# A two-layer decoder trunk on one core: x and the first weights in one array at the opening, the first norm from token rows, and the last product in two column halves

## The chip, the core and the metric

The kernel runs on one core of a Trainium2 chip. It is written in Bass with a tile framework that puts the instructions of each engine in an order at build time; on the chip each engine then runs its own list in that order. The engines are TensorE (PE, with weight loads listed as PEld), VectorE (DVE), ScalarE (ACT), GpSimd (POOL) and SyncE (SP, which here only issues DMAs). The metric is the device time of one execution in microseconds (us), lower is better.

## What is computed

The reference is a decoder trunk of two layers over 256 tokens of width 2048, float32:

```python
h = x
for layer in range(2):
    hn = rms_norm(h, norm_mix[layer])
    mix = recurrent_mixers(hn, ...) if layer % 2 == 0 else dilated_attention(hn, positions, ...)
    h = h + mix
    h = h + squared_relu_mlp(rms_norm(h, norm_mlp[layer]), mlp_w1[layer], mlp_w2[layer])
return rms_norm(h, final_norm)

def rms_norm(x, gain):
    return x * lax.rsqrt(jnp.mean(x * x, axis=-1, keepdims=True) + 1e-6) * gain

def squared_relu_mlp(h, w1, w2):
    return jnp.square(jax.nn.relu(h @ w1)) @ w2
```

Layer 0 mixes with an RG-LRU group and an HGRN2 group behind one input projection, layer 1 with dilated window attention. The width of the MLPs is 8192. Nearly all the arithmetic is matrix products with 256 rows.

## The kernel before

**Numbers and tiles.** A float32 product is made of three matmuls of a faster type: each operand is split into a rounded part and a remainder ("hi" and "lo" for weights, the two halves of bufa or bufb for activations), and hi x hi, hi x lo and lo x hi are summed in PSUM. Weights come as units of 128 x 2048 (1 MB); `fetch` loads one into `raw` (three buffers), ACT casts hi (L104), VectorE subtracts for lo (L105). hi and lo have three buffers each, so a unit's cast waits until TensorE has finished the unit three before. x is split in the same way by `split_to` with the norm's gain (ACT L252, VectorE L253); the norm's factor itself is applied to the products afterwards.

**The opening.** 12 warm-up matmuls on ones (L263) come first on TensorE. `fetch_first` then loads x by features (`xin`, 16 blocks k of 128 features by 256 tokens) and the first four weight units in alternating transfers on SP's queue: pieces of one k for the first unit, of two k's for the second, whole units after that. The first product, `v0` (L191, `tokens` with `by_k`), is 2 token halves x 512 columns over 16 k's: 24 matmuls per weight unit in the order of k, 96 in all. `FirstNorm` squares each block of xin (ACT L284), adds the squares on VectorE (L287, L289) and sums over features with matmuls against ones (L297); VectorE makes rt = 1/sqrt by Newton steps (L334 to L339), ACT scales v0 with it, and two transposes with the identity out of `tab_` (L321) turn it into the row vector `rs` that scales the products of the projections. x by tokens (`xtok`, 2 MB), the residual, is loaded over xin afterwards. All large matmuls are chained in program order (`mm`); small ones, such as those of the recurrence, are placed between them when the program is built. Projections of the recurrence stage take 48 matmuls of 256 columns and one of three PSUM banks.

**The MLP's end.** `blocks` computes two column groups of 512 (n0, n0 + 1) for two token halves j = 0, 1 with seven block products where eight would be plain: units "a", "t1", "t2", "c", "t3", "d", "t4" of 12 matmuls each, and four plain units "n" of 24 (12 for each j). The order is that of `ORDERS`; for w2 it ends t3, d, n 2, t4, n 3. `beta` and `gamma` are the PSUM banks of the first group's j = 1 and j = 0. In the last call (layer 1, q = 3, n0 = 2) column group 2 (`LAST`) is finished last. `to_x` (L769) adds a bank times the norm factor to the residual `xres`, and `Norm.add` (L308) squares 512 columns with a running sum for the final norm.

**The end.** For each j, VectorE and ACT make the final factor (L974 to L983), and four groups of 512 columns are scaled, by ACT (L992) or VectorE (L990, L996). With j = 0 ACT scales groups 0 and 3, with j = 1 groups 0 and 1. The output leaves in four pieces of 512 KB: three on SP's queue, the first half of j = 1 on ACT's.

Of the kernel before, what the change touches and what calls it, by code (L numbers as in the profile page):

```python
# [41 lines left out]
def trunk_kernel(ctx, tc, x, xtok, cols, tab, masks, pos, fin, w_in, w_gate, w_out, w_qkv, w_o, w1, w2, out):  # L42
# [17 lines left out]
    xin = xall.rearrange("p (k s) -> p k s", s=S)  # L60
# [14 lines left out]
    where = {"x": (w_in, lambda i: i, 1), "y": (w_in, lambda i: 8 + i, 1), "g": (w_gate, lambda i: i, 1),  # L75
             "v": (w_in, lambda i: 16 + 16 * i, 4), "h": (w_in, lambda i: 20 + i // 4 * 16 + i % 4 * 3, 3)}
# [16 lines left out]
    class Weights:  # L93
# [7 lines left out]
        def split(self, at, n):  # L101
            h, l = self.part(at, n)
            w = self.raw[:, at:at + n]
            A.copy(h, w)  # L104
            i = V.tensor_tensor(l, w, h.bitcast(F32), OP.subtract)  # L105
            self.ins = getattr(i, "ins", i)
# [4 lines left out]
    def fetch():  # L111
# [5 lines left out]
        with stream():  # L117
# [4 lines left out]
            nc.sync.dma_start(r, src[i])  # L122
# [154 lines left out]
    class FirstNorm:  # L277
        def __init__(self):
            self.ss, self.n = [], 0

        def add(self, blk):
            self.n += 1
            q = wk.tile([P, S], F32, name="t1", bufs=2)
            A.activation(q, blk, AF.Square)  # L284
            if self.n == 1:
                self.ss.append(wk.tile([P, S], F32, name="q", bufs=1))
                V.tensor_copy(self.ss[0], q)  # L287
            elif self.n < KB:
                V.tensor_tensor(self.ss[0], self.ss[0], q, OP.add)  # L289
            else:  # L290
                self.ss.append(q)

        def mean(self):
            p = psc.tile([P, 512], F32, name="pt", bufs=1)
            for j in range(2):
                for i, q in enumerate(self.ss):
                    T.matmul(p[:, 2 * j:2 * j + 1], q[:, j * P:j * P + P], one, start=i == 0, stop=i == 1)  # L297
            m = tmp.tile([P, 2], F32, name="nm2", bufs=2)
            V.tensor_scalar(m, p[:, 0:4:2], 1.0 / D, EPS, op0=OP.mult, op1=OP.add)
            return m  # L300

    class Norm:
        def __init__(self):
            self.ss = tmp.tile([P, 2, 4], F32, name="ss", bufs=2)

        def add(self, j, n):
            q = tmp.tile([P, S], F32, name="z").bitcast(BF16)
            A.activation(q, xres[:, j, n * 512:n * 512 + 512], AF.Square, accum_out=self.ss[:, j, n:n + 1])  # L308
# [51 lines left out]
    def tokens_group(src, i0, rt=None, by_k=False, kgs=(0, 1, 2, 3)):  # L360
        ps = tokens(src, i0, bufa, kgs, by_k)
        v = vgs.tile([P, 2, 512], F32, name="vg")
        with urgent():
            for j in range(2):
                A.activation(v[:, j], ps[j], AF.Copy, scale=1.0 if rt is None else rt[:, j:j + 1])
# [80 lines left out]
    def hgrn_v(i):  # L446
        v = tokens_group(w_in, 16 + i * 16, rt if i else None, by_k=not i)
        if not i:
            for j in range(2):
                A.activation(v[:, j], v[:, j], AF.Copy, scale=rt[:, j:j + 1])  # L450
        return v

    def hgrn(hd, vg):
        u0 = 16 + (hd // 4) * 16 + 4 + (hd % 4) * 3
# [130 lines left out]
    for step in ORDER.split():  # L585
        i = int(step[1])
        if step[0] == "v":
            vgroups[i] = hgrn_v(i)
# [68 lines left out]
    def blocks(src, i0, n0, mov, forms, events, final):  # L657
# [11 lines left out]
        def times(bank, w, get):  # L669
            for i in range(4):  # L670
                h, l = w.part(i * 512, 512)
                xh, xl = get(i)
                mm(bank, xh, h, start=not any(b is bank for b in opened), stop=False, skip_group_check=True)
                opened.append(bank)
                mm(bank, xh, l, start=False, stop=False, skip_group_check=True)
                mm(bank, xl, h, start=False, stop=i == 3, skip_group_check=True)

        plains = [0, 0]
        for what, u in ORDERS[src is not w1]:
            w = unit(src, None if u is None else i0 + 4 * n0 + u)  # L680
            due = len(later)
            if what != "n":
# [433 lines left out]
```

## Time and profile before

| | us |
|---|---|
| median of 3 runs | 2155.81 |
| lowest and highest | 2155.46, 2155.9 |
| the profiled execution | 2155.38 |
| its span, first to last instruction | 2153.4 |

The profile is of one execution. Its span is cut into windows and groups; busy time is what an engine's instructions took, "idle before" what an engine waited ahead of them and for whom. PEclk is the clock that TensorE was granted, as a share of full speed. A DMA is shown where it is issued (SPq, ACTq), and its landing is counted from there. In the timeline a row begins with its start and its duration in us; the starts of two rows of one engine give the pace, since instructions overlap at their ends.

### The profile page before, as it was taken

Reading aid. Unit: us, or ns where it says so; the run is one execution under the profiler, and the core shown is the slowest. Engines: PE = TensorE matmul, PEld = TensorE weight load, DVE = VectorE, ACT = ScalarE, POOL = GpSimd, SP = SyncE. Lnnn points to the kernel's source line nnn. Section 1 sums busy time; section 2 is a strip of 40 time slices with the busy share of each in tenths; the row PEclk is TensorE's granted clock in tenths of the full one; section 3 lists DMA queues with packets and bytes.
Section 4 is the critical chain, followed back from the end, with each engine's and each line's share of the span. In section 5 each row is a group of like instructions: output and inputs, shape, how many; then the busy total and the mean of one; then the engine's idle time right before and its main releaser. Section 6 shows DMA issues by size and latency. Waiting matters only on the chain.

```text
span 2153.4 us, 27729 instructions
## 1 busy us (share of the span) xinstructions
PE 2139.0 (99%) x11020; PEld 1831.6 (85%) x11020; DVE 1787.4 (83%) x2098; ACT 1269.8 (59%) x1415; POOL 61.9 (3%) x77
## 2 busy tenths in 40 slices
PE   9999999999999999999999999999999999999998
PEld 8999998888888888888888888888888888888886
DVE  7776787788888888889998897867988988888887
ACT  7444485566566566557665545456655755755764
POOL 0000000000000000000000000000000000000000
PEclk9999999999999999999999999999999999999999
DMA  8444446578878788887785556457878778788884
GB/s 321 157 157 158 156 157 214 177 233 272 247 243 257 256 248 238 277 247 237 236 271 197 175 159 232 157 185 224 238 239 284 238 241 262 257 246 241 274 257 154
DMA packets 68736, 485.64 MB, mean 226 GB/s; under 512 B 7664, under 2 KB 8432, under 8 KB 10624
## 3 DMA queue, kind: packets, MB, share of 16 engines
q1 hardware_dynamic: 58176, 410.89, 52.0%
q0 software_dynamic: 10144, 72.39, 18.2%
q8 instruction: 86, 1.41, 0.3%
q10 hardware_dynamic: 288, 0.61, 0.1%
q14 instruction: 42, 0.34, 0.0%
HBM read 481.76 MB, written 2.10 MB: 225 GB/s over the span
## 4 chain that ended last, share of the span: by engine, by line
PE 97%; DVE 1%; ACT 1%; DMA 0%; issue 0%; SPq 0%
PE p L191 67%; PE pd L191 13%; PE po L191 12%; PE pl L194 2%; PE pl L487 1%; PE pt L191 1%; DVE lo L105 0%; DMA xall<-in_x 0%; PE pl L883 0%; ACT hi L104 0%; PE po L904 0%; PE pd L896 0%; PE pd L471 0%; PE pl L882 0%; PE po L905 0%
## 5 line engine op out<-in xcount | busy, mean ns | idle before, releaser
L104 ACT CAST hi<-raw 128x2048 fp32r<-128x2048 f32 (+2 forms) x468 | 683.7, 1484 | 546.9 <-PE p L191 343.0
L105 DVE TENSOR_TENSOR lo<-raw,hi 128x2048 fp32r<-128x2048 f32 (+2 forms) x468 | 816.3, 1759 | 218.5 <-ACT hi L104 203.6
L191 PE MATMUL p<-hi,bufb 128*128 128x512 f32 x1408 | 448.8, 391 | 0.5 <-ACT bufb L249 0.5
L191 PE MATMUL p<-hi,bufa 128*128 128x512 f32 x1136 | 365.3, 391 | 0.8 <-ACT hi L104 0.8
L191 PE MATMUL p<-bufa,hi 128*128 128x256 f32 (+1 forms) x1792 | 365.3, 317 | 0.1
L191 PEld LDWEIGHTS p<-hi,bufb 128*128 128x128 f32 x1408 | 264.3, 188 | 55.7 <-ACT bufb L249 0.7
L191 PEld LDWEIGHTS p<-bufa,hi 128*128 128x128 f32 x1792 | 294.2, 190 | 18.6 <-DVE hz L429 0.3
L191 PE MATMUL p<-lo,bufb 128*128 128x512 f32 x704 | 274.2, 390 | 0.0
L191 PE MATMUL p<-bufa,lo 128*128 128x256 f32 x1152 | 256.6, 287 | 0.0
L191 PEld LDWEIGHTS p<-hi,bufa 128*128 128x128 f32 x1136 | 214.0, 188 | 45.3 <-ACT hi L104 1.2
L105 DVE TENSOR_TENSOR lo<-s,hi 128x2048 fp32r<-128x2048 f32 x102 | 233.0, 2285 | 14.5 <-ACT hi L104 12.4
L104 ACT CAST hi<-s 128x2048 fp32r<-128x2048 f32 x102 | 195.1, 1913 | 51.0 <-PE po L191 22.2
L191 PE MATMUL p<-lo,bufa 128*128 128x512 f32 x568 | 222.3, 391 | 1.3 <-DVE lo L105 1.3
L191 PEld LDWEIGHTS p<-bufa,lo 128*128 128x128 f32 x1152 | 189.7, 191 | 2.7
L191 PEld LDWEIGHTS p<-lo,bufb 128*128 128x128 f32 x704 | 132.2, 188 | 26.9
L191 PEld LDWEIGHTS p<-lo,bufa 128*128 128x128 f32 x568 | 107.0, 188 | 24.7 <-DVE lo L105 2.9
L191 PE MATMUL pd<-hi,bufa 128*128 128x512 f32 x288 | 95.2, 392 | 0.0
L191 PE MATMUL p<-hi,formx 128*128 128x512 f32 x288 | 94.8, 390 | 0.0
L105 DVE TENSOR_TENSOR lo<-t,hi 128x2048 fp32r<-128x2048 f32 x34 | 77.7, 2287 | 13.0 <-ACT hi L104 13.0
L191 PE MATMUL po<-hi,bufa 128*128 128x512 f32 x256 | 84.9, 393 | 0.0
L191 PE MATMUL p<-hi,formh 128*128 128x512 f32 x256 | 84.0, 389 | 0.0
L191 PE MATMUL pd<-hi,bufb 128*128 128x512 f32 x256 | 83.0, 389 | 0.0
(302 smaller groups left out, 2888.0 us busy)
## 6 DMA issues: line engine op xcount, KB each, us to landing
raw<-in_w SPq DMA_DIRECT2D x224, 1024.0 KB, 6.6
raw<-in_w_in SPq DMA_DIRECT2D x46, 1024.0 KB, 4.9
raw<-in_w_qkv SPq DMA_DIRECT2D x46, 1024.0 KB, 5.0
t<-in_w SPq DMA_DIRECT2D x32, 1024.0 KB, 6.7
t<-in_w POOLq DMA_DIRECT2D x32, 1024.0 KB, 8.9
s<-in_w POOLq DMA_DIRECT2D x32, 1024.0 KB, 9.2
raw<-in_w_out SPq DMA_DIRECT2D x16, 1024.0 KB, 4.9
raw<-in_w_o SPq DMA_DIRECT2D x16, 1024.0 KB, 4.9
```

Of the source, the lines that this page charges most:

```text
L104: A.copy(h, w)
L105: i = V.tensor_tensor(l, w, h.bitcast(F32), OP.subtract)
L191: chain[:] = [after(T.matmul(*args, **kw), chain)]
L194: chain[:] = [after(T.transpose(out_, in_, ident), chain)]
L487: T.matmul(pl[:, j], kq[:, js], halves(qp[:, js], c, True), start=True, stop=True)
```

## The change

At the opening, x and the first two weight units are packed on the host into one array `head`, [128, 8, 256 + 512], so that one DMA brings a block k of x and its weights; the first four k's come one by one, the next four in pairs, into a buffer `both_in` that is given back afterwards. The other half of x goes to `x_in`. The constants `tab_` and `msk` are loaded later, behind the second token half. `FirstNorm` is gone: the token rows (`xtok`) are loaded in two halves earlier, ACT squares each half with a running sum, and rt comes from that. The order on ACT and SP is held by `after`: first half's square ahead of the eviction of v0, second half's load behind a weight unit. There are 9 warm-up matmuls in place of 12.

At the end, the last call of `blocks` takes n 3 before t4. t4 is computed in two halves of 256 columns: the first into beta, which is then finished by `to_x` (512 columns, of which the second half still lacks t4), the second into a bank of its own, `rest`, added to the residual by a shorter instruction with its own square. The scaling of the output is dealt out so that ACT has groups 0 and 3 and VectorE 1 and 2 for both j, two waits that ordered it are dropped, and the second half of j = 1 goes on ACT's queue instead of the first.

The core of the diff:

```diff
+    openers = ExitStack()
+    opening = openers.enter_context(tc.tile_pool(name="opening", bufs=1))
+    both_in = opening.tile([P, 8, S + 512], F32, name="both_in")
+    x_in = opening.tile([P, 8, S], F32, name="x_in")
+
     units = []
     made = {}
+    loads, casts = [], []
+    order_of = lambda src, i: ORDERS[0 if src is w1 else 2 if src is w2 and i == 120 else 1]
+
     def plan2(src, i):
-        for what, u in ORDERS[src is not w1]:
+        for what, u in order_of(src, i):
             units.append((src, None if u is None else i + u, what, i))
...
-        def split(self, at, n):
+        def split(self, at, n, w=None):
             h, l = self.part(at, n)
-            w = self.raw[:, at:at + n]
-            A.copy(h, w)
+            if w is None:
+                w = self.raw[:, at:at + n]
+            else:
+                h, l = (t.rearrange("p (k c) -> p k c", c=512) for t in (h, l))
+            casts[:] = [after(A.copy(h, w), [])]
             i = V.tensor_tensor(l, w, h.bitcast(F32), OP.subtract)
...
             at[0] += 1
+            if u < 2:
+                made[u] = Weights(None, 0)
+                m = u + 1
+                for k in range(4 * u, 4 * u + 4, m):
+                    nc.sync.dma_start(both_in[:, k:k + m], head[:, k:k + m])
+                    for i in range(k, k + m):
+                        split_to(bufa[:, i], both_in[:, i, :S], col("nmix0", i))
+                    made[u].split((k - 4 * u) * 512, m * 512, both_in[:, k:k + m, S:])
+                continue
             r = wraw.tile([P, 2048], F32, name="raw")
             src, i = units[u]
-            n = (4, 2, 1, 1)[u]
-            for m in range(n):
-                ks = slice(4 * u + m * 4 // n, 4 * u + (m + 1) * 4 // n)
-                ws = slice(m * 2048 // n, (m + 1) * 2048 // n)
-                nc.sync.dma_start(xin[:, ks], x[:, ks])
-                nc.sync.dma_start(r[:, ws], src[i][:, ws])
-                if m == 0 and n > 1:
-                    made[u] = Weights(r, 0)
-                for k in range(ks.start, ks.stop):
-                    split_to(bufa[:, k], xin[:, k], col("nmix0", k))
-                if n > 1:
-                    made[u].split(m * 2048 // n, 2048 // n)
-                else:
-                    made[u] = Weights(r, 1024)
+            made[u] = Weights(r, 0)
+            nc.sync.dma_start(x_in[:, 4 * u - 8:4 * u - 4], x[:, 4 * u - 8:4 * u - 4])
+            n = 1024 if u == 2 else 2048
+            for m in range(0, 2048, n):
+                nc.sync.dma_start(r[:, m:m + n], src[i][:, m:m + n])
+            for m in range(2):
+                for k in range(4 * u + 2 * m, 4 * u + 2 * m + 2):
+                    split_to(bufa[:, k], x_in[:, k - 8], col("nmix0", k))
+                made[u].split(1024 * m, 1024)
...
-    nc.sync.dma_start(tab_, tab)
     msk = cst.tile([P, NLEV, P], I8, name="msk")
-    nc.sync.dma_start(msk, masks)
...
-    class FirstNorm:
-        def __init__(self):
...
-                self.ss.append(wk.tile([P, S], F32, name="q", bufs=1))
-                V.tensor_copy(self.ss[0], q)
-            elif self.n < KB:
-                V.tensor_tensor(self.ss[0], self.ss[0], q, OP.add)
-            else:
-                self.ss.append(q)
-
-        def mean(self):
-            p = psc.tile([P, 512], F32, name="pt", bufs=1)
-            for j in range(2):
-                for i, q in enumerate(self.ss):
-                    T.matmul(p[:, 2 * j:2 * j + 1], q[:, j * P:j * P + P], one, start=i == 0, stop=i == 1)
-            m = tmp.tile([P, 2], F32, name="nm2", bufs=2)
...
+    openers.close()
     vgs = mixers.enter_context(tc.tile_pool(name="vgs", bufs=1))
     wk = mixers.enter_context(tc.tile_pool(name="wk", bufs=2))
-    nrm = FirstNorm()
-    for k in range(KB):
-        nrm.add(xin[:, k])
-    rt = rstd(nrm)
+    fetch()
+    halfs = [after(nc.sync.dma_start(xres[:, 0], xtok[:, 0]), loads)]
+    m = tmp.tile([P, 2], F32, name="nm2", bufs=2)
+
+    def square(j):
+        q = wk.tile([P, 4, S], F32, name="gr", bufs=1).rearrange("p m s -> p (m s)").bitcast(BF16)
+        return after(A.activation(q, xres[:, j], AF.Square, accum_out=m[:, j:j + 1]), casts[-1:] if j else [])
+
+    halfs.append(square(0))
+    vfirst = tokens_group(w_in, 14, by_k=True, behind=halfs[1:])
+    load = after(nc.sync.dma_start(xres[:, 1], xtok[:, 1]), loads)
+    for d, f in ((tab_, tab), (msk, masks)):
+        load = after(nc.sync.dma_start(d, f), [load])
+    square(1)
+    V.tensor_scalar(m, m, 1.0 / D, EPS, op0=OP.mult, op1=OP.add)
+    rt = tmp.tile([P, 2], F32, name="nr2", bufs=2)
+    rsqrt(rt, m, 2)
+    for j in range(2):
+        A.activation(vfirst[:, j], vfirst[:, j], AF.Copy, scale=rt[:, j:j + 1])
     rs = tmp.tile([P, S], F32, name="nr", bufs=1)
     A.copy(rs, over_tokens(rt))
-    nc.sync.dma_start(xres, xtok)
...
-        def times(bank, w, get):
+        def times(bank, w, get, at=0, m=512, out_=None):
+            out_ = bank if out_ is None else out_
             for i in range(4):
-                h, l = w.part(i * 512, 512)
+                h, l = w.part(i * 512 + at, m)
                 xh, xl = get(i)
-                mm(bank, xh, h, start=not any(b is bank for b in opened), stop=False, skip_group_check=True)
+                mm(out_, xh, h, start=not any(b is bank for b in opened), stop=False, skip_group_check=True)
                 opened.append(bank)
-                mm(bank, xh, l, start=False, stop=False, skip_group_check=True)
-                mm(bank, xl, h, start=False, stop=i == 3, skip_group_check=True)
+                mm(out_, xh, l, start=False, stop=False, skip_group_check=True)
+                mm(out_, xl, h, start=False, stop=i == 3, skip_group_check=True)
-        plains = [0, 0]
-        for what, u in ORDERS[src is not w1]:
+        plains, did = [0, 0], []
+        for what, u in order_of(src, i0 + 4 * n0):
             w = unit(src, None if u is None else i0 + 4 * n0 + u)
             due = len(later)
-            if what != "n":
+            did.append(what)
+            if what == "t4" and plains[0] == 2:
+                times(beta, w, side[what], 0, S, beta[:, :S])
+                final(0, 1, beta)
+                rest = psc.tile([P, 512], F32, name="pt", bufs=1)
+                times(rest, w, side[what], S, S, rest[:, :S])
+                events["rest"](rest[:, :S])
+            elif what != "n":
...
                     times(sums[n, j], w, lambda i, j=j, g=g: plain(j, 4 * g + i))
-                    if plains[n] == 2:
+                    if plains[n] == 2 and (n, j, "t4" in did) != (0, 1, False):
                         final(n, j, sums[n, j])
...
                 if nrm and last:
-                    nrm.add(j, n)
+                    nrm.add(j, n, 0, S if ending and (j, n) == (1, LAST) else 512)
+
+        ending = nrm and not nrm.next
+        ends = {}
+
+        def rest(bank):
+            x_ = xres[:, 1, LAST * 512 + S:LAST * 512 + 512]
+            with urgent():
+                V.scalar_tensor_tensor(x_, bank, r2[:, 1:2], x_, op0=OP.mult, op1=OP.add)
+                nrm.add(1, LAST, S, S, nrm.rest)
+
+        if ending and n0:
+            nrm.rest = tmp.tile([P, 1], F32, name="fs", bufs=1)
+            ends["rest"] = rest
...
-    fnorm = Norm()
...
-    roots, sums2, rr = [], [], []
+    rr = []
...
-            i = V.scalar_tensor_tensor(m, ss[:, LAST:LAST + 1], 1.0 / D, m, op0=OP.mult, op1=OP.add)
-            sums2.append(getattr(i, "ins", i).name)
-            i = A.activation(t, m, AF.Sqrt)
-            roots.append(getattr(i, "ins", i).name)
+            V.scalar_tensor_tensor(m, ss[:, LAST:LAST + 1], 1.0 / D, m, op0=OP.mult, op1=OP.add)
+            if j:
+                V.scalar_tensor_tensor(m, fnorm.rest, 1.0 / D, m, op0=OP.mult, op1=OP.add)
+            A.activation(t, m, AF.Sqrt)
...
         for j in range(2):
-            for n, e in ((0, A), (LAST, V), (1, A if j else V), (3, V if j else A)):
+            for n, e in ((0, A), (1, V), (3, A), (LAST, V)):
...
                 elif e is A:
-                    i = A.activation(x_, x_, AF.Copy, scale=rr[j])
-                    if n == 3:
-                        after(i, roots[1:])
+                    A.activation(x_, x_, AF.Copy, scale=rr[j])
                 else:
-                    i = V.tensor_scalar(x_, x_, rr[j], None, op0=OP.mult)
-                    if n == 1:
-                        after(i, sums2[1:])
+                    V.tensor_scalar(x_, x_, rr[j], None, op0=OP.mult)
             for h in range(2):
                 at = slice(h * 1024, h * 1024 + 1024)
-                (nc.scalar if j and not h else nc.sync).dma_start(out[:, j, at], xres[:, j, at])
+                (nc.scalar if j and h else nc.sync).dma_start(out[:, j, at], xres[:, j, at])
...
-WARM = 12
+WARM = 9
...
-ORDERS = (_A + (("n", 6),) + _B + (("n", 7),) + _C, _A + (("n", 7),) + _B + (("n", 6),) + _C)
+ORDERS = (_A + (("n", 6),) + _B + (("n", 7),) + _C, _A + (("n", 7),) + _B + (("n", 6),) + _C,
+          _A + (("n", 7),) + _B + (("n", 6), ("t3", None), ("d", 1), ("n", 2), ("n", 3), ("t4", None)))
...
+    xf = n(a["x"]).reshape(S, KB, P).transpose(2, 1, 0)
+    head = np.concatenate([xf[:, :8], fv[:2].reshape(2, P, 4, 512).transpose(1, 0, 2, 3).reshape(P, 8, 512)], axis=2)
...
-        "x": c(n(a["x"]).reshape(S, KB, P).transpose(2, 1, 0)),
+        "head": c(head), "x": c(xf[:, 8:]),
```

In the order in which the program is built, the two transposes for `rs` stand behind the second projection of the recurrence stage, small matmuls of that stage stand a little later between the large ones than before, and from the end of that stage to the last call of `blocks` TensorE's list is the same.

More of the change, by code (lines that the diff above doesn't have):

```diff
@@ L41, in trunk_kernel @@
 @with_exitstack
-def trunk_kernel(ctx, tc, x, xtok, cols, tab, masks, pos, fin, w_in, w_gate, w_out, w_qkv, w_o, w1, w2, out):
+def trunk_kernel(ctx, tc, head, x, xtok, cols, tab, masks, pos, fin, w_in, w_gate, w_out, w_qkv, w_o, w1, w2, out):
     nc = tc.nc
@@ L121, in fetch @@
             r = wraw.tile([P, 2048], F32, name="raw")
-            nc.sync.dma_start(r, src[i])
+            loads[:] = [after(nc.sync.dma_start(r, src[i]), [])]
             made[u] = Weights(r, 1024)
@@ L358, in tokens, with tokens_group @@
         return ps
-    def tokens_group(src, i0, rt=None, by_k=False, kgs=(0, 1, 2, 3)):
+    def tokens_group(src, i0, rt=None, by_k=False, kgs=(0, 1, 2, 3), behind=()):
         ps = tokens(src, i0, bufa, kgs, by_k)
@@ L364, in tokens_group @@
             for j in range(2):
-                A.activation(v[:, j], ps[j], AF.Copy, scale=1.0 if rt is None else rt[:, j:j + 1])
+                after(A.activation(v[:, j], ps[j], AF.Copy, scale=1.0 if rt is None else rt[:, j:j + 1]), behind)
         return v
@@ L444, in halves @@
         return t.rearrange("p (n two c) -> p n two c", two=2, c=c)[:, :, int(second), :]
[L446 to L451, printed above, removed]
     def hgrn(hd, vg):
-        u0 = 16 + (hd // 4) * 16 + 4 + (hd % 4) * 3
+        u0 = 18 + (hd // 4) * 16 + (hd % 4) * 3
         oml = omlb[:, hd:hd + 1]
@@ L784, in second @@
                {"a": lambda b: to_x(b, 0, n0, r2, False), "t1": lambda b: to_x(b, 1, n0 + 1, r2, False),
-                "t2": u2, "t3": u3},
+                "t2": u2, "t3": u3, **ends},
                lambda n, j, b: to_x(b, j, n0 + n, r2, (n, j) != (1, 1)))
```

24 lines of the change are left out of this document (9 added, 15 removed).

## The prediction

> **What bounds the kernel now.** The page comes first. Its busy shares say which engine sets the time.
>
> ```profile
> span 2153.4 us, 27729 instructions
> PE 2139.0 (99%) x11020; PEld 1831.6 (85%) x11020; DVE 1787.4 (83%) x2098; ACT 1269.8 (59%) x1415; POOL 61.9 (3%) x77
> ```
>
> TensorE is idle for 2153.4 - 2139.0 = 14.4 us in all, so apart from the number of matmuls only those 14.4 us, and matmuls that run slowly, can be won. The change touches the two ends, so next come the stage windows of the opening (columns: stretch, its length, busy time and starts of PE, PEld, DVE, ACT, POOL, then granted clock, DMA share, GB/s), the second group for the warm-up matmuls of L263 alone, and TensorE's timeline.
>
> ```profile
> 4.40:7.81 3.41, 2.90 (x18) 2.21 (x16) 3.41 (x17) 2.89 (x9) 0.00 (x0) 1.00 0.90 280
> 7.81:11.22 3.41, 3.41 (x15) 2.27 (x14) 3.26 (x13) 2.67 (x7) 0.00 (x0) 1.00 1.04 357
> 11.22:14.63 3.41, 1.89 (x8) 1.02 (x8) 3.28 (x10) 3.41 (x9) 0.00 (x0) 1.00 1.06 430
> 14.63:18.04 3.41, 3.41 (x9) 2.63 (x10) 3.41 (x10) 3.34 (x8) 0.00 (x0) 0.51 1.01 420
> 18.04:32.29 14.25, 14.25 (x64) 11.80 (x63) 14.23 (x32) 11.75 (x19) 0.00 (x0) 1.00 0.86 325
> ...
> 1.06:4.40 3.34, 3.34 (x15) 3.34 (x16) 1.00 0.71 200
> 4.40:5.38 0.98, 0.98 (x11) 0.98 (x9) 1.00 0.85 270
> ```
>
> ```profile
> 5.38 0.50 PE L191 MATMUL p<-hi,bufa 128*128 128x512 f32 x1
> ...
> 12.08 0.40 PE L191 MATMUL p<-hi,bufa 128*128 128x512 f32 x1
> 13.23 0.50 PE L191 MATMUL p<-hi,bufa 128*128 128x512 f32 x1 [0.76 <-ACT hi L104]
> 14.49 0.64 PE L191 MATMUL p<-lo,bufa 128*128 128x512 f32 x1 [0.76 <-DVE lo L105]
> ...
> 32.29 0.40 PE L191 MATMUL p<-bufa,hi 128*128 128x256 f32 x2
> ```
>
> The first product (96 matmuls, four weight units of 24, k by k) begins at 5.38 and the next product at 32.29: 26.91 us. The chain of waits gives the undisturbed pace and one more thing on TensorE's path, the eight passes of the first norm's sum (L297):
>
> ```profile
> 34.13 0.79 PE pt L297 x8
> ...
> 52.34 4.19 PE p L191 x35
> ...
> 2138.13 2.72 PE p L191 x12
> ```
>
> A 512-column matmul takes 2.72 / 12 = 0.227 us, a 256-column one 4.19 / 35 = 0.120. So 96 need 21.8 us and the opening loses 5.1: its operands come too late up to 14.5, and from 14.63 to 18.04 the granted clock is 0.51 (9 starts in 3.41 us, where 15 fit). What makes the operands late is VectorE, 3.41 of 3.41 us busy, then 3.26. One k on it, and the same operations on both engines:
>
> ```profile
> 8.82 0.69 DVE L105 TENSOR_TENSOR lo<-raw,hi 128x512 fp32r<-128x512 f32 x1
> 9.43 0.16 DVE L401 TENSOR_SCALAR e<-e 128x8 f32<-128x8 f32 x1
> 9.50 0.48 DVE L253 SCALAR_TENSOR_TENSOR bufa<-xall,c__83,bufa 128x256 fp32r<-128x256 f32 x1
> 9.90 0.42 DVE L289 TENSOR_TENSOR q<-q,t 128x256 f32<-128x256 f32 x1
> 10.23 0.16 DVE L423 TENSOR_TENSOR lb<-lb,ex 128x8 f32<-128x8 f32 x1
> 10.31 0.68 DVE L105 TENSOR_TENSOR lo<-raw,hi 128x512 fp32r<-128x512 f32 x1
> ```
>
> ```profile
> L104 ACT CAST hi<-raw x14: 602/1040/1051, 4.7 to 29.3; 128x1024 fp32r<-128x1024 f32 x10, 128x512 fp32r<-128x512 f32 x4
> L105 DVE TENSOR_TENSOR lo<-raw,hi x14: 682/1212/1224, 5.7 to 31.5; 128x1024 fp32r<-128x1024 f32 x10, 128x512 fp32r<-128x512 f32 x4
> ...
> L252 ACT ACTIVATE bufa<-xall,c__83 x16: 492/493/512, 4.2 to 21.6; 128x256 fp32r<-128x256 f32 x16
> ...
> L284 ACT ACTIVATE t<-xall x16: 399/402/422, 3.9 to 27.7; 128x256 f32<-128x256 f32 x16
> ```
>
> From start to start a k costs VectorE 10.31 - 8.82 = 1.49 us, TensorE six matmuls, 1.36. Of the 1.49 the norm's addition is 0.33 (9.90 to 10.23).
>
> The tail, by timeline, and the window in which the output moves:
>
> ```profile
> 2140.89 0.75 DVE L769 SCALAR_TENSOR_TENSOR xall<-p,nm,xall 128x512 f32<-128x512 f32 x1 [5.43 <-PE p L191]
> ...
> 2143.18 0.39 PE L191 MATMUL po<-hi,bufb 128*128 128x512 f32 x1
> 2143.31 0.16 DVE L982 SCALAR_TENSOR_TENSOR ft<-ft,fm 128x1 f32<-128x1 f32 x1
> 2143.61 0.75 DVE L769 SCALAR_TENSOR_TENSOR xall<-po,nm,xall 128x512 f32<-128x512 f32 x1
> 2144.45 0.63 ACT L308 ACTIVATE z<-xall 128x512 bf16<-128x512 f32 x1 [1.57 <-DVE fr L983]
> ...
> 2144.99 0.19 ACT L308 ACTIVATION_READ_ACCUMULATOR z<-xall 128x1 f32 x1
> ...
> 2145.83 2.37 SPq L1001 DMA_DIRECT2D out<-xall  x3
> ...
> 2146.50 0.16 DVE L983 SCALAR_TENSOR_TENSOR fr<-ft,fr 128x1 f32<-128x1 f32 x1
> 2146.69 1.33 ACT L992 ACTIVATE xall<-xall,fr 128x512 f32<-128x512 f32 x2 [0.20 <-DVE fr L983]
> 2148.06 0.35 ACTq L1001 DMA_DIRECT2D out<-xall  x1
> ```
>
> ```profile
> 2146.55:2151.80 5.25, 0.00 (x0) 0.00 (x0) 1.26 (x3) 1.33 (x2) 0.00 (x0) 0.64 0.99 396
> ```
>
> The last matmul ends at 2143.57, 9.8 us before the end of the span. From 2146.55 to 2151.80 the DMA engines are full (share 0.99): the four output pieces, 2.1 MB at 396 GB/s, take 5.25 us whatever is computed meanwhile. The end is therefore the first output's issue (2145.83), 0.72 until it flows, 5.25, and 1.60 after the last byte.
>
> **The opening, worked out.** The change takes off ACT 16 squares (0.40 each), off DVE a copy and 14 additions, off TensorE the L297 passes, and off the front of SP's queue the two constant loads (340 KB). x and weights of one k come in one transfer (384 KB, rows of 3 KB), of two k's after the fourth. ACT squares the token rows twice later (2048 columns each; twice a 1024-column cast, 1.04, gives 2.1 us each, behind covered casts).
>
> Landing: the rows show this for the first k before.
>
> ```profile
> xall<-in_x SPq DMA_DIRECT2D x1, 128.0 KB, 3.1
> ...
> raw<-in_w_in SPq DMA_DIRECT2D x1, 256.0 KB, 3.4
> ```
>
> Issued at 0.74 and 1.18, these landed at 3.84 and 4.58. The same bytes in one transfer issued at 0.74 land between; I take 4.1. Rates were 280 GB/s with rows of 1 and 2 KB, 430 with 4 and 8 KB; for 3 KB I take 360, for 6 KB 420. So k1 to k3 land at 5.2, 6.3, 7.4, the pairs at 9.3 and 11.2.
>
> ACT: cast 0.60 and split 0.49 make the first matmul start at 5.2 (5.38 before). VectorE then needs 1.49 - 0.33 = 1.16 us a k with two small operations, so k0 to k3 are supplied about as fast as TensorE takes them, and it has done them at 11.2. The first pair: landed 9.3, two splits 0.9, one 1024-column cast 1.0, its remainder on DVE 1.15: 12.35. TensorE stands about 1 us there. The pairs behind are in time (k6 ready 14.3, wanted 15.0; k8 ready 17.2, wanted 17.7; k12 ready 21.2, wanted 23.1), so 71 matmuls x 0.227 = 16.1 follow and the next product starts at 28.4: **3.9 us** earlier. Bounds: never waiting, 5.2 + 21.8 = 27.0 gives 5.3; all landing at 280 GB/s (pair at 11.0, start 30.1) and a halved window (below) on top gives 0.7. I stay at 3.9: the nearest rows are the 4 KB ones.
>
> L297 gone: **0.8 us**, on TensorE's own path. The turning of the norm over tokens stays, two products later in TensorE's order; it needs the constants and both token halves, which are 12 MB down a stream of 400 GB/s, about 30 us, while the vector is first missed when the fourth projection wants a bank: 28.4 + 3 x 48 x 0.120 = 45.7. The new waits on ACT (square behind the first token half, with the eviction of the first product and the next cast queued behind it) cost nothing while that half lands before the product ends: 8.4 MB at 400 GB/s is 23 us against 28.4.
>
> The clock: the halved stretch is 3.41 us long; stepping back by that gives 11.22, 7.81, 4.40, and at 4.40 the warm-up's pace changes too (15 starts in 3.34 us, then 11 in 0.98). A stretch with 8 starts (1.89 busy) was followed by half clock, one with 18 (2.90) was not. After the change 4.40 to 7.81 has the last 3 warm-up passes and about 10 matmuls, 11.22 to 14.63 about 10: nearer the good row, so I count no halved stretch. The Trainium skill ("TensorE: Matmul & The Clock Gate", section "Why this matters for your kernels") asks only that idle gaps stay under about 3 us. This trace disagrees: the two waits before the half clock were 0.76 us each. By that rule the sum stays as it is.
>
> **The tail.** The two-bank split alone is small: twelve 512-column matmuls become 24 of 256, 24 x 0.120 - 2.72 = +0.16. What counts is that token half 1's last product now comes after n 3, so half 0 is final 12 x 0.227 + 2.88 = 5.6 us before the last matmul instead of 2.73. Its chain (update from 2140.89, square, root, factor, of which the last step but one begins at 2143.31 and the last would take 0.16 more, were VectorE not taken by half 1's update) takes 2.8 us when nothing lies in the way and two scalings on each engine 1.4, so its two outputs are issued 2.1 and 1.3 us before the last matmul ends, and their 2.6 us of flow leave the tail. Half 1: update of 256 columns 0.45 (0.48 in the row of L253, 0.75 for 512 columns), square 0.40 + 0.19, then the root chain, 1.2, which in before stood behind a scaling: factor 2.3 us after the last matmul (3.1 before). Scaling on both engines at once: first piece issued at 3.0, second at 3.7; 0.72 and 2 x 1.31 of flow: 6.35. Before: 2151.80 - 2143.57 = 8.23. So 1.9 - 0.16 = **1.7 us**. Bounds: 0.6 if only the shorter chain counts, 2.2 if both pieces flow at once.
>
> **The sum.** 3.9 + 0.8 + 1.7 = 6.4. The profiled execution took 2155.38 us, 2.0 more than its span: 2149.0. The median run is 0.43 above it: **2149.4**. In the middle TensorE idles only 14.4 - 1.1 - 2.0 - 9.8 = 1.5 us, so nothing is won there; small products of the recurrence stage change places, for which I allow 1 us either way.
>
> **Rivals.** (1) The clock. Nine warm-up matmuls, 18 passes, last until about 4.7 instead of 5.4. If the gate counts 4.40 to 7.81 as too idle, 7.81 to 11.22 runs 9 matmuls instead of 15: 1.4 us; if the first stretch is half as well, 2.0, of which 1.0 at most hides in the wait at the first pair. Result 2150.4 to 2151.4. For it: fewer starts than in the good row; against: 13 is well over 8. Chance 0.17. The same page and section ask for at least 4 us of warming; 15 passes at 0.22 and 3 faster ones make 3.6, so by it this rival would be the forecast. The trace's pace changed after 3.34 us, which speaks against it.
> (2) Transfers bind: landings at 280 GB/s, opening gains 2.2: 2151.1; with half the tail's gain 2152. Chance 0.10. For it: DMA share 0.90 to 1.06 all through; against: rates rose with row length.
> (3) The tail's order does not help, because half 0's chain waits on ACT or DVE behind other work: only 0.6 there, 2150.5. Chance 0.06.
> (4) Slower: ACT waits for the token halves in order, ahead of the eviction and of the casts for the second and third projection. TensorE wants the second one's weights at 34.2; after the first half lands ACT and DVE need 2.1 + 1.3 + 1.0 + 1.2 = 5.6, so each us of landing after 28.6 is a us lost. To end over 0.2% slower it must eat 6.4 + 4.3, landing at 39: 8.4 MB at 230 GB/s. The rows show no such rate once rows are long: 0.06, 2160.
>
> **Numbers.** Forecast 0.61 (2148.3 to 2150.7). 0.2%, 4.3 us, is about what a measurement of this kernel can tell from no change: under 2151.5 is faster. All of the forecast, most of (1) and (3) and half of (2) lie there, 0.87; I take 0.07 off for what no row shows, above all the recurrence stage: 0.80, same 0.13, slower 0.07. The range 2147.3 to 2152.6 reaches to the better bounds (8.3 in all: 2147.5) and holds cases 1 to 3.
>
> **What would show it.** Right: next product starting at 28 to 29; granted clock 1.00 throughout; VectorE under 90% busy from 4.4 to 11; one TensorE wait of about 1 us at the fifth k; half 0's outputs issued before the last matmul; last byte some 6.4 us after it. Wrong: PEclk 0.5 in any window, ACT waiting on the token load past 28, TensorE waits near the first heads, or outputs still flowing back to back after the last matmul.

## The result, and the profile after

The changed kernel takes 2162.15 us (median of 8 runs, 2161.98 to 2162.54) against 2155.52 for the kernel before beside it: ratio 1.0031, 95% interval 1.0022 to 1.0040. It is slower, by 6.6 us; 2149.4 was forecast, in a range up to 2152.6. The profiled execution took 2162.02 us. First the page's head:

```profile
span 2160.2 us, 27708 instructions
...
PE 2147.0 (99%) x11018; PEld 1829.7 (85%) x11018; DVE 1785.5 (83%) x2085; ACT 1268.6 (59%) x1405; POOL 61.9 (3%) x77
```

TensorE is busy 8.0 us longer than before (2139.0), with two fewer matmuls. Its idle time fell from 14.4 to 13.2 us. So nothing waits more than before: matmuls themselves take longer.

**The opening** in stage windows (columns as in the prediction), then single rows of the timeline:

```profile
4.40:7.81 3.41, 2.42 (x12) 1.56 (x10) 2.90 (x14) 3.00 (x8) 0.00 (x0) 1.00 1.02 387
7.81:11.22 3.41, 3.41 (x17) 2.79 (x16) 3.38 (x18) 2.52 (x6) 0.00 (x0) 1.00 1.00 416
11.22:14.63 3.41, 2.54 (x11) 1.75 (x10) 3.38 (x11) 3.38 (x7) 0.00 (x0) 1.00 0.97 360
14.63:18.04 3.41, 3.41 (x16) 2.82 (x15) 3.41 (x9) 3.41 (x7) 0.00 (x0) 1.00 1.03 430
```

```profile
4.71 0.62 ACT L115 CAST hi<-both_in 128x512 fp32r<-128x512 f32 x1 [2.04 <-DMA both_in<-in_head]
...
5.79 0.50 PE L206 MATMUL p<-hi,bufa 128*128 128x512 f32 x1 [0.87 <-ACT bufa L267]
...
13.17 0.50 PE L206 MATMUL p<-lo,bufa 128*128 128x512 f32 x1 [0.86 <-DVE lo L116]
...
29.40 0.40 PE L206 MATMUL p<-bufa,hi 128*128 128x256 f32 x2
```

No halved stretch is there (16 starts from 14.63 on, where before had 9), and inside the product one wait of 0.86 us is left, at the fifth k. The next product starts at 29.40, 2.9 us earlier than before.

**The middle.** The same 24 products of an MLP stage, first and one past the last, before and then after (timeline of TensorE):

```profile
437.80 0.39 PE L191 MATMUL pd<-hi,formx 128*128 128x512 f32 x1
...
443.24 0.39 PE L191 MATMUL p<-hi,bufa 128*128 128x512 f32 x1
```

```profile
434.02 0.39 PE L206 MATMUL pd<-hi,formx 128*128 128x512 f32 x1
...
439.61 0.39 PE L206 MATMUL p<-hi,bufa 128*128 128x512 f32 x1
```

After is 3.8 us ahead when they begin, but they take 5.59 us where they took 5.44, with no wait in either. The groups by shape show which matmuls are slower (busy us, then mean ns of one; before, then after). The names behind the arrow are the moving operand, which streams through the array, and the stationary one, which is loaded into it:

```profile
L191 PE MATMUL p<-hi,bufb 128*128 128x512 f32 x1408 | 448.8, 391 | 0.5 <-ACT bufb L249 0.5
...
L191 PE MATMUL p<-hi,formx 128*128 128x512 f32 x288 | 94.8, 390 | 0.0
...
L191 PE MATMUL p<-hi,formh 128*128 128x512 f32 x256 | 84.0, 389 | 0.0
```

```profile
L206 PE MATMUL p<-hi,bufb 128*128 128x512 f32 x1408 | 449.2, 391 | 0.5 <-ACT bufb L264 0.5
...
L206 PE MATMUL p<-hi,formx 128*128 128x512 f32 x288 | 96.6, 396 | 0.0
...
L206 PE MATMUL p<-hi,formh 128*128 128x512 f32 x256 | 85.6, 395 | 0.0
```

Only those with formx or formh (the forms of `blocks`) as stationary operand are slower, by 6 ns each. From start to start, over all of them, it is 0.2268 us before and 0.2330 after. 1632 matmuls read a form. By the trace's start times the intervals that begin with one of them have grown by 9.9 us in all, those that lead into a stretch of them by 0.7 and those just behind a stretch by 0.3: 10.9 us. By the last matmul (2151.54 against 2143.57) the 3.8 us of lead have become 8.0 us of lag, 0.16 of it the split last product, so the middle lost 11.6 us.

The diff has one line that no step of the prediction mentions: `nrm.rest = tmp.tile([P, 1], F32, name="fs", bufs=1)`, a tile of 4 bytes. In the built program's memory map it takes a slot of 32 bytes in the pool `tmp`, and each tile of a pool opened later lies 32 bytes further: formx at 167776 instead of 167744 bytes in each partition, formh at 200544 instead of 200512. bufa (24896), bufb (57664) and the weights' buffers (hi from 115008, lo from 139584) stay.

**The tail** (timeline, then windows):

```profile
2148.80 1.34 ACT L1011 ACTIVATE xall<-xall,fr 128x512 f32<-128x512 f32 x2 [0.81 <-DVE fr L1002]
...
2149.55 5.43 SPq L1016 DMA_DIRECT2D out<-xall  x3
...
2151.26 0.28 PE L206 MATMUL pt<-hi,bufb 128*128 128x256 f32 x1
...
2153.71 0.16 DVE L1002 SCALAR_TENSOR_TENSOR fr<-ft,fr 128x1 f32<-128x1 f32 x1
...
2155.27 0.35 ACTq L1016 DMA_DIRECT2D out<-xall  x1
```

```profile
2155.40:2158.00 2.60, 0.00 (x0) 0.00 (x0) 0.00 (x0) 0.00 (x0) 0.00 (x0) 0.50 0.97 392
2158.00:2158.20 0.20, 0.00 (x0) 0.00 (x0) 0.00 (x0) 0.00 (x0) 0.00 (x0) 0.50 0.41 144
2158.20:2158.40 0.20, 0.00 (x0) 0.00 (x0) 0.00 (x0) 0.00 (x0) 0.00 (x0) 0.50 0.01 0
```

Half 0 is scaled and its first output issued before the last matmul ends (2151.54). The span ends 8.66 us after that, 9.83 before the change.

### The profile page after: what moved, and what is told of

The parts are those of the page before. It is cut to its first block, busy times and chain, and to the rows that moved or that the text cites. A ratio compares the mean times of both kernels' runs of the same rounds, so it can differ in the third digit from the quotient of the medians.

```text
span 2160.2 us, 27708 instructions
## 1 busy us (share of the span) xinstructions
PE 2147.0 (99%) x11018; PEld 1829.7 (85%) x11018; DVE 1785.5 (83%) x2085; ACT 1268.6 (59%) x1405; POOL 61.9 (3%) x77
## 4 chain that ended last, share of the span: by engine, by line
PE 97%; DVE 1%; ACT 1%; DMA 0%; issue 0%
PE p L206 67%; PE pd L206 13%; PE po L206 12%; PE pl L209 2%; PE pl L485 1%; PE pt L206 1%; DVE lo L116 1%; PE pl L902 0%; ACT hi L115 0%; PE po L923 0%; PE pd L915 0%; DMA both_in<-in_head 0%; PE pd L469 0%; PE pl L901 0%; PE po L924 0%
## 5 line engine op out<-in xcount | busy, mean ns | idle before, releaser
L115 ACT CAST hi<-raw 128x2048 fp32r<-128x2048 f32 (+1 forms) x462 | 679.0, 1493 | 569.9 <-PE p L206 344.6
L116 DVE TENSOR_TENSOR lo<-raw,hi 128x2048 fp32r<-128x2048 f32 (+1 forms) x462 | 810.4, 1771 | 214.3 <-ACT hi L115 197.4
```

The costliest lines, as they stand in the source:

```text
L115: casts[:] = [after(A.copy(h, w), [])]
```

## The experiments

The kernel before ran beside each group: 2155.3 to 2155.6 us.

**1. Undo the shift, or do the shift alone.** The first kernel is the changed one with the small sum in a spare word of r2n; the second is the kernel before with a tile that nobody reads; the third and fourth move formh alone.

```diff
 e1: -  nrm.rest = tmp.tile([P, 1], F32, name="fs", bufs=1)
     -  r2n = tmp.tile([P, 2], F32, name="r2n", bufs=2)
     +  r2n = tmp.tile([P, 3], F32, name="r2n", bufs=2)
     +  nxt.rest, r2n = r2n[:, 2:3], r2n[:, :2]
 e2: +  V.memset(tmp.tile([P, 1], F32, name="fs", bufs=1), 0.0)
 e3: -  return pool_, pool_.tile([P, 4, 2, 512], F32R, name="formh")
     +  h = pool_.tile([P, 4096 + 16], F32R, name="formh")
     +  return pool_, h[:, 8:8 + 4096].rearrange("p (m t c) -> p m t c", m=4, t=2)
 e4: as e3, h[:, 4:4 + 4096]
```

> The changed kernel with one difference: the 4-byte sum of the last half group lies in a spare word of the r2n tile instead of in a tile fs of its own, so that formx and formh lie at 167744 and 200512 bytes again, as before the change, and not 32 bytes further. Theory (a matmul whose stationary operand lies at an odd multiple of 32 bytes takes 0.0063 us longer, and some 1632 such matmuls read formx or formh): about 11 us less than the changed kernel, 2150 to 2152 us; rows with formx and formh go from 0.233 back to 0.227 us from start to start. Rival (the opening, the new order of the last product or the instructions beside TensorE slow the middle): 2161 to 2163 us, as the changed kernel.

> The kernel before with one added tile of 4 bytes in the pool tmp, cleared once and not read: it has the old opening and the old last product, and formx and formh lie 32 bytes further. Theory (address of the stationary operand): 10 to 11.5 us more than the kernel before, 2165.5 to 2167 us. Rival (opening, last product or other instructions of the change): 2155 to 2156 us.

> The kernel before with formh alone starting 32 bytes into its tile (200544 instead of 200512); formx, t1 and s stay where they were. Theory (address of the stationary operand, by matmul): some 768 matmuls read formh, at 0.0063 us each 4.8 us, 2160.3 us; rows with formx stay at 0.227 us. Rival (it is the other tiles that moved, or the two forms together): 2155 to 2156 us.

> As the run with formh 32 bytes further, but with formh starting 16 bytes into its tile (200528). If only the odd multiple of 32 bytes costs: 2155 to 2156 us. If every start off a multiple of 64 bytes costs the same: 2160.3 us. If the number of pieces of a weight row that cross a boundary counts, more than that or something between.

Measured: e1 2150.93 us (ratio to before 0.9979, 0.9970 to 0.9988); e2 2166.79 (1.0053, 1.0041 to 1.0066); e3 2160.69 (1.0025, 1.0016 to 1.0034); e4 2155.55 (1.0002, 0.9993 to 1.0011). Groups of e1, then of e3:

```profile
L206 PE MATMUL p<-hi,formx 128*128 128x512 f32 x288 | 94.8, 390 | 0.0
...
L206 PE MATMUL p<-hi,formh 128*128 128x512 f32 x256 | 84.0, 389 | 0.0
```

```profile
L191 PE MATMUL p<-hi,formx 128*128 128x512 f32 x288 | 94.9, 390 | 0.0
...
L191 PE MATMUL p<-hi,formh 128*128 128x512 f32 x256 | 85.6, 395 | 0.0
```

The address is the cause: the change without the shift is 4.4 us faster than before, the shift without the change 11.5 slower, and moving one of the two forms slows that one alone. 16 bytes cost nothing.

**2. Which operand's address?** An unread 4-byte tile (a slot of 32 bytes) in pool `act`, behind bufb or ahead of bufa.

```diff
 e6:    bufb = act.tile([P, KB, 2 * S], F32R, name="bufb")
     +  nc.vector.memset(act.tile([P, 1], F32, name="fs"), 0.0)
 e7: +  nc.vector.memset(act.tile([P, 1], F32, name="fs"), 0.0)
        bufa = act.tile([P, KB, 2 * S], F32R, name="bufa")
```

> The kernel before with the unread tile of 4 bytes behind bufb: bufa and bufb stay at multiples of 64 bytes, the weights' tiles raw, hi and lo and everything behind them (formx and formh too) lie 32 bytes further. Theory A (the address of the stationary operand by itself): as the run that moved only what lies behind tmp, 2166.8 us, and on top of it what the 512 products of 512 columns with hi as stationary operand (512 x 0.0063 = 3.2 us) and some 2500 products of 256 columns cost (0 to 16 us): 2167 to 2186 us; rows with bufa and bufb as stationary operand stay at 0.227 us. Theory R (stationary and moving operand at different places in a block of 64 bytes): formx and formh now agree with hi and lo and go back to 0.227 us, but the 5448 products with bufa or bufb as stationary operand go to 0.233 us, 34 us, with 3 to 19 us for those where hi or lo is stationary: 2190 to 2209 us.

> The kernel before with the unread tile of 4 bytes ahead of bufa: bufa, bufb, raw, hi, lo, formx and formh all lie 32 bytes further. Theory A (the address of the stationary operand by itself): the 5448 products with bufa or bufb as stationary operand cost 0.0063 us more each, 34 us, on top of what the run with the tile behind bufb gives: 2201 to 2220 us. Theory R (the two operands' places differ): they agree everywhere, 2155 to 2156 us.

Measured: e6 2189.33 us (1.0157, 1.0143 to 1.0171), e7 2155.94 (1.0001, 0.9992 to 1.0010). Groups of e6:

```profile
L192 PE MATMUL p<-hi,bufb 128*128 128x512 f32 x1408 | 456.7, 396 | 0.5 <-ACT bufb L250 0.5
L192 PE MATMUL p<-hi,bufa 128*128 128x512 f32 x1136 | 371.2, 396 | 0.9 <-ACT hi L105 0.8
...
L192 PE MATMUL p<-hi,formx 128*128 128x512 f32 x288 | 95.0, 390 | 0.0
```

The products of the projections in e6, whose stationary operand is hi, by columns:

```profile
L192 PE MATMUL p<-bufa,hi 128*128 128x256 f32 x1280 | 236.9, 284 | 0.1
L192 PE MATMUL p<-bufa,hi 128*128 128x512 f32 x512 | 128.2, 399 | 0.0
```

My theory, the stationary operand's own address, falls; theory R holds, though e6 lies 0.7 us under its range: it had allowed 3 to 19 us for products with hi or lo as stationary operand, and only the 512-column ones are slower (395 ns before), not those of 256 columns (286). In e6 bufa and bufb lie where they always did and are slow, because hi and lo have moved away from them, and the shifted forms are fast, because hi and lo moved with them. In e7 everything has moved together and nothing is slower. What counts is the difference of the two operands' addresses. The loading of the next stationary operand takes part in it: in after the product just ahead of a stretch of forms, whose own two operands agree, takes 235 ns from start to start (227 before).

**3. Which differences?** Three kernels spread the four blocks of formh (each read by 192 products) by another pitch; four move formh as a whole, another way in each layer.

```diff
 e10: +  h = pool_.tile([P, 4, 1024 + 12], F32R, name="formh")
      +  return pool_, h[:, :, :1024].rearrange("p m (t c) -> p m t c", t=2)
 e11: 1024 + 10;  e12: 1024 + 24
 e14: +  h, at = pool_.tile([P, 4096 + 128], F32R, name="formh"), (16, 32)[layer]
      +  return pool_, h[:, at:at + 4096].rearrange("p (m t c) -> p m t c", m=4, t=2)
 e15: (12, 24);  e16: (6, 10);  e17: (64, 128)
```

> The kernel before with the four blocks of formh 48 bytes further apart, so that block k begins at 0, 48, 96 and 144 bytes against its old place, in a block of 64 bytes at 0, 48, 32 and 16. Each block is read by 192 products. The two operands' places in a block of 64 bytes matter (theory R, confirmed by the runs with the tile ahead of and behind bufa and bufb). If only a difference of exactly 32 bytes costs: block 2 alone at 0.233 us, the others at 0.227, 1.2 us in all. If every difference from 32 to 63 costs: blocks 1 and 2, 2.4 us. If a difference that is no multiple of 32 costs in part: block 1 between 0.227 and 0.233.

> As the run with 48 bytes, with the blocks of formh 40 bytes further apart: places 0, 40, 16 (80) and 56 (120) in a block of 64 bytes. If only a difference of exactly 32 costs: no block slower, 0 us. If every difference from 32 to 63 costs: blocks 1 and 3 at 0.233 us, 2.4 us.

> As the run with 48 bytes, with the blocks of formh 96 bytes further apart: 0, 96, 192 and 288 bytes from the old place. If the period is 64 bytes: blocks 1 and 3 at 0.233 us, blocks 0 and 2 at 0.227, 2.4 us in all. If the period is 128 bytes (cost at 32 alone): block 3 alone, 1.2 us; if it is longer, or the places are not what counts, none or all four.

> The kernel before with formh as a whole 64 bytes from its old place in layer 0 and 128 bytes in layer 1; some 384 products read it in each layer (2.4 us for a layer at 0.0063 us each). The runs with stretched pitch slowed blocks at differences of 48, 80, 120, 144, 192 and 288 bytes, which a period of 64 bytes does not give. If the period is 64 and those runs are slow by carry-over from one block to the next: both layers at 0.227 us, 2155 to 2156 us. If the difference counts up to a longer period: 64 slow, 2157.7 us, or 64 and 128 slow, 2160 us.

> As the run with 64 and 128 bytes, with 48 in layer 0 and 96 in layer 1. Period 64 with a difference of exactly 32 dear: layer 0 at 0.227 us, layer 1 at 0.233, 2157.7 us. The upper half of a block of 64 dear, or every difference above 16 up to a longer period: both at 0.233 us, 2160 us.

> As the run with 64 and 128 bytes, with 24 in layer 0 and 40 in layer 1. Differences of 0 and 16 were free and 32 cost 0.0063 us. The upper half of a block of 64 dear: layer 0 free, layer 1 dear, 2157.7 us. Every difference above 16 dear: both, 2160 us. Only 32 dear: none, 2155.3 us.

> As the run with 64 and 128 bytes, with 256 in layer 0 and 512 in layer 1. In the kernel before, every stationary and every moving operand lies at the same place in a block of 512 bytes. If the period is 512: layer 0 at 0.233 us, layer 1 at 0.227, 2157.7 us. If it is 256 or shorter: none, 2155.3 us. If longer: both, 2160 us.

Measured, one run each: e10 2160.20, e11 2158.55, e12 2158.32 us. e10 and e11 are slower than each of their expectations and e12 lies between the price of two slow blocks and of four, since blocks at 80, 120, 144, 192 and 288 bytes were slow (0.232 to 0.234 from start to start). So a period of 64 bytes was wrong. Then e14 2161.75, e15 2161.05, e16 2157.90, e17 2156.22 (0.85 us above before, all of it there when the second product starts, at 33.14 against 32.29, long before formh is read). Start to start of the products with formh, from the trace's start times, some 350 for each place:

| bytes off | 0 | 16 | 24 | 32 | 40 | 48 | 64 | 96 | 128 | 256 | 512 |
|---|---|---|---|---|---|---|---|---|---|---|---|
| ns | 226.8 | 226.9 | 230.6 | 233.0 | 228.2 | 233.3 | 233.5 | 234.3 | 232.8 | 226.9 | 226.8 |

The groups of formh say the same in mean ns: e14 over both layers, then e17, then e16 in layer 0 (300 to 1100 us) and layer 1 (1400 to 2150):

```profile
L191 PE MATMUL p<-hi,formh 128*128 128x512 f32 x256 | 85.7, 395 | 0.0
```

```profile
L191 PE MATMUL p<-hi,formh 128*128 128x512 f32 x256 | 84.0, 389 | 0.0
```

```profile
L191 PE MATMUL p<-hi,formh 128*128 128x512 f32 x128 | 42.5, 392 | 0.0
```

```profile
L191 PE MATMUL p<-hi,formh 128*128 128x512 f32 x128 | 42.2, 390 | 0.0
```

256 and 512 bytes are free, everything tried from 32 to 128 costs 6 to 7.5 ns save 40, and 24 and 40 cost part, which none of e16's three expectations has. That fits a period of 256 bytes, in which the kernel before has all its large operands at the same place (64). Between 128 and 256 no whole tile was tried, and 192 only in a run with another pitch. Why 40 costs less than 32 stays open, and so does what couples the two reads.

**4. The two parts alone, without the small tile.** e8 has the new opening and the old last product; e9 has the old opening and the last product of e1. Their edits in words:

```diff
 e8: the change, but ORDERS[src is not w1], fnorm = Norm(), the old times() and the old output loop
 e9: the change's ORDERS, times(), rest() and output loop on the old opening, the sum in r2n
```

> The kernel before with the opening of the changed kernel alone (x and first weights in one array, norm by tokens, 9 warm-up products), the old last product, no tile fs, so formx and formh at their old places. If opening and last product add up: the run with the sum in a spare word gave -4.4 us against the kernel before, of which the trace shows 3.3 at the end of the recurrence stage and 2.7 between the last product stage's start and the last matmul; so the opening gives about -3.3 us, 2151.5 to 2152.5 us. If the opening works against the middle stages: 2154 us or more.

> The kernel before with the new order of the last product, its two halves and the new output alone; the old opening; the sum in a spare word, so formx and formh at their old places. If the two parts add up: -0.5 to -2 us against the kernel before, 2153.3 to 2154.8 us. If the new order of the last product costs as much as it saves: 2155 to 2156 us.

Measured: e8 2152.52 us (0.9986, 0.9977 to 0.9994), e9 2154.52 (0.9996, 0.9987 to 1.0005). -3.1 and -1.1 add up to about e1's -4.4; the interval of the tail alone includes no change.

**5. The warm-up.** e1 with 4 warm-up products instead of 9.

```diff
-WARM = 9
+WARM = 4
```

> The changed kernel with the sum in a spare word of r2n, and 4 warm-up products in place of 9. If the clock is granted by how busy the last stretches were (the theory of the prediction's first rival): the warm-up ends at about 2.8 us, the first product begins at 5.7 as before, a stretch of 3.41 us of the first product runs at granted clock 0.5, and the kernel takes 1.4 to 2 us more than with 9: 2152.3 to 2153 us. If the warm-up has no effect on the clock: 2150.5 to 2151.3 us, as with 9.

Measured: 2151.54 us (0.9982, 0.9973 to 0.9992), between the two theories. TensorE's timeline:

```profile
8.19 1.05 PE L206 MATMUL p<-hi,bufa 128*128 128x512 f32 x2
9.04 0.63 PE L206 MATMUL p<-lo,bufa 128*128 128x512 f32 x1
...
12.47 0.39 PE L206 MATMUL p<-lo,bufa 128*128 128x512 f32 x1
12.70 0.61 PE L206 MATMUL p<-hi,bufa 128*128 128x512 f32 x2
```

From 8.19 to 9.04 two matmuls begin, 0.43 us apart; from 12.47 to 12.70 it is 0.23. The first matmuls run at half pace, but that costs less than forecast, since the fifth k is then asked for so late that its wait is gone: the next product starts at 30.61, against 29.44 in e1. The ten runs lie between 2151.11 and 2151.97, the profiled one (2151.97) at the upper end.

## Why the prediction was wrong

**The step that failed** is the middle: TensorE idles there for only 1.5 us, "so nothing is won there", with 1 us allowed either way for the recurrence stage. That counts waits alone. The middle lost 11.6 us without a wait, 10.9 of them at the matmuls that read a form, because the 4-byte tile had moved the forms by 32 bytes. The prediction's own first reading said what else could move the time, "matmuls that run slowly", and no step then asked whether any would. None of the rivals is what happened; the 0.07 for slower rested on ACT waiting for the token halves, and ACT waited for them 0.5 us in all, once (waits of after: total, times, longest):

```profile
ACT gr L375 <- DMA xall<-in_xtok: 0.5, 1, 0.5
```

With the sum in a spare word (e1) the same change takes 2150.93 us, 1.5 above the forecast and inside its range. It gains 4.4 us on the kernel before beside it where 6.4 was forecast, so the steps on the two ends had the right sign and were too large in sum.

**The opening**: 3.9 + 0.8 was forecast; at the first form products 3.8 us is there in after, 3.3 in e1 and 2.9 in e8, one execution each. The next product starts at 29.40 instead of 28.4, because the wait at the fifth k ends at 13.17 instead of 12.35: the first k's transfer lands at about 4.7 (ACT's cast, freed by the DMA) where I took 4.1, between two smaller ones, and the first pair as much later, at 9.9 instead of 9.3 (ACT's splits of it):

```profile
9.91 0.91 ACT L267 ACTIVATE bufa<-both_in,c__88 128x256 fp32r<-128x256 f32 x2 [0.83 <-DMA both_in<-in_head]
```

The other 0.2 is the splits, the cast and the remainder behind it. The rate and the "one wait of about 1 us at the fifth k" were right. That VectorE would fall under 90% busy was wrong: 2.90 and 3.38 of 3.41 us in the two windows from 4.40 to 11.22, 92%.

**The clock**: no PEclk is below 1.00 until after the last matmul. But the halved stretch of before was a trait of that execution and not of the old opening: of the 13 other runs with the old opening only e17's trace has one (15.68 to 19.10), and in the other twelve the next product starts at 31.6 to 32.9, on both sides of before's 32.29. And e8, with the new opening and the same 9 warm-up products, has a stretch from 7.81 to 11.22 nearly as slow as the rival's 9 matmuls in its profiled execution (window, then timeline; the first row of the timelines is the warm-up, after's ahead of e8's):

```profile
7.81:11.22 3.41, 3.41 (x11) 2.71 (x10) 3.38 (x18) 2.22 (x5) 0.00 (x0) 1.00 1.00 395
```

```profile
1.05 3.87 PE L278 MATMUL po<-ones 128*128 128x128 f32 x18 [1.05 <-DVE e L403]
```

```profile
1.05 4.21 PE L276 MATMUL po<-ones 128*128 128x128 f32 x18 [1.05 <-DVE e L399]
...
8.98 0.63 PE L204 MATMUL p<-lo,bufa 128*128 128x512 f32 x1
9.40 1.05 PE L204 MATMUL p<-hi,bufa 128*128 128x512 f32 x2
10.26 0.49 PE L204 MATMUL p<-lo,bufa 128*128 128x512 f32 x1
```

11 starts where after has 17. The column's 1.00 means nothing there: these traces hold the granted clock only from its first change on, and windows ahead of that are shown as 1.00. The first record is at 4.42 us in after, 5.80 in e1, 10.47 in e8 and 11.94 in e13 (4.00 to 7.26 in the runs with 12 warm-up products), and in e8 and e13 the pace doubles there. So the clock did not fall, as the rival had it, but rose late. The same 18 passes take 3.87 us in after, whose last ones are already at full pace, and 4.21 in e8, whose matmuls are still 0.43 apart at 9.40. Its next product starts at 29.86, so this cost 0.5 us against after, not 1.4 to 2.0. The Trainium skill ("TensorE: Matmul & The Clock Gate", section "What's actually happening") says that the window of the clock gate runs freely and that the change falls at another point from run to run, within 500 ns; these two executions agree that it moves, but by more, 4.42 against 10.47 us. Reading one trace's 3.34 us as the length of warming that suffices was the error there.

**The tail**: 1.7 forecast, 1.0 measured in after (9.83 - 8.66, less 0.16). The factor 2.3 us and the second output's issue 3.7 us after the last matmul were right to 0.1. The last bytes begin to flow 3.9 after it instead of 3.7, take 2.8 instead of 2.6, and the span ends 2.0 after them instead of 1.6. Most of the shortfall belongs to the opening: from the last matmul to the end of the span it is 9.8 us in every run with both old parts, 8.1 with the new last product alone (e9), 10.4 with the new opening alone (e8) and 8.6 with both (e1). So beside either opening the new last product takes 1.7 to 1.8 us off, less 0.16, near the forecast, and the new opening adds 0.5 behind the last output byte; why stays open. Of e9's gain 0.4 is lost outside the span, which is 2.4 us shorter than the time (2154.18 - 2151.8) where before's is 2.0 shorter, and its median gained only 1.1.

## What to carry to other kernels

Where TensorE is busy 99%, ask of each edit what it does to the length of a matmul, not only to waits; a new tile of a few bytes in a pool opened early moves every later tile, so compare the memory maps of the two programs as one compares their instruction orders. Keep the stationary and the moving operand of 512-column matmuls at the same place within 256 bytes (a period that fits every distance tried here), put small tiles into spare words or behind the large ones, and, when a change loses time evenly with no wait to show for it, compare mean durations by shape and operand first.

## What the runs showed of the hardware that was not expected

- A 512-column matmul of this kernel goes from 0.2268 to 0.2330 us, 2.7%, when the addresses of its two operands differ by 32 bytes, and a kernel in which nearly all of them do loses 33.7 us (e6). Its 256-column matmuls are no slower there (284 ns against 286). The Trainium skill ("TensorE: Matmul & The Clock Gate", section "Step-by-step: what each phase is for") says that loading the next weights takes no read bandwidth from the running matmul, by two independent read ports. Here the pace depends on the two addresses together, so the measurement limits that sentence.
- TensorE's first microseconds can run at half pace (0.427 us from start to start in e8 and e13) while the granted clock is shown as 1.00, because the trace has no record of the clock before its first change (10.47 and 11.94 us there); the starts in a window tell, the column does not.
